# Modulation in steps of two slabs at every second place, and choice tables held in PSUM

## The chip, the cores and the metric

One core of a Trainium2 chip runs the whole program in one launch. The metric is the device time in microseconds (us), median of several executions. Before: 2350.81 us, the median of 3 executions from 2339.59 to 2353.79.

## What is computed

A two-layer backbone over 256 latent tokens (stream x) and 256 context tokens (stream c), width 1024. Each layer mixes tokens with four mixers (windowed attention, gated delta rule, latent attention, retention) and then channels: a dense SwiGLU in layer 0, the best two of eight experts in layer 1. Every sub-layer is modulated by rows that come from a product with `w_mod`:

```python
for layer in range(DEPTH):
    mod_x = (silu_c @ w_mod[layer] + b_mod[layer])[:, None, :]
    mod_c = silu_cc @ w_mod[layer] + b_mod[layer]
    sh1_x, sc1_x, g1_x, sh2_x, sc2_x, g2_x = jnp.split(mod_x, 6, axis=-1)
...
logits = (x @ w_router).astype(jnp.float32)
top_val, top_idx = lax.top_k(logits, TOP_K)
gates = jax.nn.softmax(top_val, axis=-1)
combine = jnp.sum(jax.nn.one_hot(top_idx, N_EXPERTS, dtype=jnp.float32) * gates[..., None], axis=1)
for e in range(N_EXPERTS):
    out = out + combine[:, e:e + 1].astype(x.dtype) * swiglu(x, w_gate[e], w_up[e], w_down[e])
```

## The kernel before, in words

**Long products.** Weights arrive as float32 slabs of 256 rows by 512 columns (512 KB, tile `raw`, five buffers, all loads issued on SP's queue). ScalarE rounds each half to `hi` (lines 200 and 225), VectorE forms the rest `lo` (lines 201 and 226), and TensorE makes three products of the parts (lines 183 to 185). A dense SwiGLU works through seven hidden groups of 512: four slabs of the gate weights (`fg_dram`), two times two of the up weights (`fu_dram`), two times two of the down weights (`fd_dram`). Results are summed in PSUM tiles `acc`, which come from two rings of two banks.

**Modulation between them.** The product with `w_mod` has 24 chunks of 512 columns over both layers. Four chunks are made at the start by `mod`; the other 20 (8 in layer 0, 12 in layer 1) are made in small steps between the slabs of the long products. A step is one `w_mod` slab of 256 rows: `mod_part` (line 285 on) loads it into a buffer of `raw` (line 287) and multiplies it into a PSUM tile `modp` (line 292; 8 calls, which the trace shows as 16 matmul records). VectorE then copies (line 325) or adds (line 327) `modp` to the row tile `mrow` in SBUF. After four steps `mod_out` turns the row (line 297) and adds the bias (line 298). `tick`, which the loops over slabs call at fixed places, takes one step from the list `Fill.steps`; `need_mod` takes steps at once until a chunk is done. `modp` takes its bank from the ring of `acc` that the running product does not use. A dense hidden group has four places, so one chunk is made in each.

**Route.** After the last output projection, `route` (line 1549 on) makes the router's logits `lg`, finds the best two of eight experts per token, and ranks the tokens of each expert. The tables are 128 x 2 x 8 or smaller, in SBUF: `lg` (lines 1563 and 1586), `top` (1574), `eq` (1577), `first` (1579), `hot` (1581), their sum `sel` (1587), the counts `prk` by two matmuls (1589, 1591), and `rank` (1592). `pick` compares `rank` with a row of numbers and gives the selection matrix `oh` (1649); `gather` (1661) multiplies with it the normed tokens, split into `hnh` and `hnl`. The parts `hnl` are made by GpSimd (line 1569) while VectorE makes the choice. `weights` (lines 1597 to 1606: `dl`, `w`, `cw`, `cwt`) makes the experts' weights beside it. Then come the experts: 1 MB slabs `eraw` in nine buffers, split on lines 1624 and 1625, products `gu` and `pd`.

**What sets the order.** A list scheduler places each engine's instructions in advance; work inside `soon()` has priority, `mod_step` and `weights` have none. Each engine works strictly in the placed order, and so does SP with its loads.

Of the kernel before, what the change touches and what calls it, by code (L numbers as in the profile page):

```python
# [11 lines left out]
F32 = mybir.dt.float32  # L12
# [3 lines left out]
OP = mybir.AluOpType  # L16
# [9 lines left out]
OFF = 1024.0  # L26
# [44 lines left out]
def bc(ap, pos, n):  # L71

    a = list(ap.ap)
    a.insert(pos, [0, n])
    return bass.AP(tensor=ap.tensor, offset=ap.offset, ap=a)
# [3 lines left out]
def tile_backbone(ctx: ExitStack, tc: tile.TileContext, x, ctxs, cT, w_mod, w_in, w_out, w_q_up, w_kv_up,  # L79
                  fg, fu, fd, router, mg, mu, md, rows, cols, cst, fnorm, out):  # L80
    nc = tc.nc
    V, S, T, G = nc.vector, nc.scalar, nc.tensor, nc.gpsimd
# [39 lines left out]
    class Thread:  # L122
# [5 lines left out]
        def ps(self, name="acc"):  # L128
            return pp.tile([128, 512], F32, name=name, tag=self.psum[0], bufs=self.psum[1])
# [32 lines left out]
    def soon():  # L162

        return tc.high_priority(offset=6000)

    def hv(ap, h=4):
        return ap.rearrange("p (h d) -> p h d", h=h)
# [117 lines left out]
    def mod_part(l, n, a, p, k0, k1):  # L285
        r = raw.tile([128, 2, 512], F32, name="raw", tag="raw")
        nc.sync.dma_start(r, w_mod[l, a * 256:(a + 1) * 256, n * 512:(n + 1) * 512].rearrange(
            "(k p) c -> p k c", p=128))
        for j in range(2):
            k = a * 2 + j  # L290
            for g in range(4):
                T.matmul(p[32 * g:32 * g + 32, 0:128], sct[:, k, :], r[:, j, g * 128:(g + 1) * 128],
                         start=k == k0, stop=k == k1, skip_group_check=True)

    def mod_out(l, n, row, bank=ps):
        q = bank("modc")
        T.transpose(q[:, 0:128], row, ident)
        V.tensor_tensor(MOD[l][:, 4 * n:4 * n + 4, :], hv(q[:, 0:128])[:, :, 0:2],
                        bc(CL[l]["b_mod"][:, 4 * n:4 * n + 4], 2, 2), op=OP.add)
# [20 lines left out]

    def mod_step(l, n, a):
        p = ps("modp")
        mod_part(l, n, a, p, 2 * a, 2 * a + 1)
        if a == 0:
            V.tensor_copy(mrow, p[:, 0:128])
        else:
            V.tensor_tensor(mrow, mrow, p[:, 0:128], op=OP.add)

    class Fill:

        steps, out = [], None

    def put_fill(l, chunks):
        Fill.steps += [(l, n, a) for n in chunks for a in range(4)]

    def tick():
        if Fill.out:
            mod_out(*Fill.out, mrow)
            Fill.out = None
        if Fill.steps:  # L340
            l, n, a = Fill.steps.pop(0)
            mod_step(l, n, a)
            if a == 3:
                Fill.out = l, n

    def need_mod(l, n):
        while Fill.out or any(st[0] == l and st[1] <= n for st in Fill.steps):
            tick()

    SI = {"x": 0, "c": 1}  # L350

    def modcol(l, kind, s):
        return MOD[l][:, kind * 8:kind * 8 + 8, SI[s]]
# [1011 lines left out]
    first = []  # L1365
# [67 lines left out]
    def squares(n, junk):  # L1433
        for t in range(2):
            S.activation(junk("junk"), H["x", t][:, n * 512:(n + 1) * 512], AF.Square,
                         accum_out=ss[:, n * 2 + t:n * 2 + t + 1])

    def turned(n, psum, sbuf):
        us = []
        for k2 in (2 * n, 2 * n + 1):  # L1440
            p = psum("utp")
            for j in range(2):
                for t in range(2):
                    T.transpose(p[:, j * 256 + t * 128:j * 256 + t * 128 + 128],
                                H["x", t][:, (2 * k2 + j) * 128:(2 * k2 + j + 1) * 128], ident)
            us.append(sbuf("u"))
            if k2 % 2:
                V.tensor_copy(us[-1], p)
            else:
                S.copy(us[-1], p)  # L1450
        return us

    def logits(n, us, acc):
        for i in range(4):
            k = 4 * n + i
            for t in range(2):
                o_ = i % 2 * 256 + t * 128
                T.matmul(acc[:, t * 8:t * 8 + 8], us[i // 2][:, o_:o_ + 128], rt[:, 1, k, :],
                         start=i == 0 and t == 0, stop=i == 3, skip_group_check=True)
# [55 lines left out]
    def pt_(name):  # L1515
        return ptr.tile([128, 512], F32, name=name, tag="tr")
# [4 lines left out]
    def sh_(name, dtype=F32):  # L1521
        return ew.tile([128, 512], dtype, name=name, tag="w")

    def e3(name, dtype=F32):
        return e0.tile([128, 2, NE], dtype, name=name, tag=name)

    def col2(name):
        return e0.tile([128, 2], F32, name=name, tag=name)

    def norms(ss):  # L1530
        ms = small(ST, 2, "ms")
        V.tensor_tensor(ms, ss[:, 0:2], ss[:, 2:4], op=OP.add)  # L1532
        V.tensor_scalar(ms, ms, 1.0 / D, EPS, op0=OP.mult, op1=OP.add)  # L1533
        return rsq(ST, ms, 2)
# [5 lines left out]
    rank, sel, cw = e3("rank"), e3("sel", F32R), e3("cw")  # L1540
# [8 lines left out]
    def route():  # L1549

        cnt = sh_("cnt", F32R)
        S.copy(cnt[:, 0:128], C["strict"])
        S.copy(cnt[:, 128:256], ones)
        squares(1, sh_)
        plg = pt_("plg")
        logits(1, turned(1, pg_, sh_), plg)
        r = norms(ss)
        V.tensor_scalar(fa[1], H["x", 1], r[:, 1:2], None, op0=OP.mult)
        lg0, lgr = e3("lg0"), e3("lgr")
        for t in range(2):  # L1560
            V.scalar_tensor_tensor(lgr[:, t], lga[:, t], r[:, t:t + 1], lsh, op0=OP.mult, op1=OP.add)
        for t in range(2):
            V.scalar_tensor_tensor(lg0[:, t], plg[:, t * 8:t * 8 + 8], r[:, t:t + 1], lgr[:, t], op0=OP.mult, op1=OP.add)
        S.mul(fa[0], H["x", 0], r[:, 0:1])
        for a in range(2):
            cc = slice(a * 512, a * 512 + 512)
            for t in (1, 0):
                S.copy(hn[0][a][t], fa[t][:, cc])
                G.tensor_tensor(hn[1][a][t], fa[t][:, cc], hn[0][a][t].bitcast(F32), op=OP.subtract)
        hot, top = [], []  # L1570
        cur = lg0
        for i in range(2):
            m = col2(f"top{i}")
            V.tensor_reduce(m, cur, axis=AX.X, op=OP.max)
            q = e3(f"eq{i}")
            for t in range(2):
                V.scalar_tensor_tensor(q[:, t], cur[:, t], m[:, t:t + 1], C["rev8"], op0=OP.is_equal, op1=OP.mult)
            f = col2(f"first{i}")
            V.tensor_reduce(f, q, axis=AX.X, op=OP.max)
            oh = e3(f"hot{i}")  # L1580
            V.tensor_tensor(oh, bc(C["rev8"], 1, 2), bc(f, 2, NE), op=OP.is_equal)
            hot.append(oh)
            top.append(m)
            if i == 0:
                cur = e3("lg1")
                V.scalar_tensor_tensor(cur, oh, -3e38, lg0, op0=OP.mult, op1=OP.add)
        V.tensor_tensor(sel, hot[0], hot[1], op=OP.add)
        prk = pt_("prk")
        T.matmul(prk[:, 0:16], cnt[:, 0:128], sel.rearrange("p t e -> p (t e)"), start=True, stop=False,
                 skip_group_check=True)  # L1590
        T.matmul(prk[:, 8:16], cnt[:, 128:256], sel[:, 0], start=False, stop=True, skip_group_check=True)
        V.scalar_tensor_tensor(rank, sel.bitcast(F32), -OFF, hv(prk[:, 0:16], 2), op0=OP.mult, op1=OP.add)
        return hot, top, cnt

    def weights(hot, top, cnt):
        dl = col2("dl")
# [42 lines left out]
                beats.remove(b)  # L1639
                b[1]()  # L1640

    def pick(e, rnd):

        oh = sh_("oh", F32R)
        rk = rank
        if rnd:
            rk = e3("rank1")
            V.tensor_scalar(rk, rank, -128.0, None, op0=OP.add)
        V.tensor_tensor(oh.rearrange("p (t i c) -> p t i c", t=2, i=2), bc(bc(C["iota"], 1, 2), 1, 2),
                        bc(rk[:, :, e:e + 2], 3, 128), op=OP.is_equal)  # L1650
        return oh
# [23 lines left out]
    def back(oh):  # L1675

        pt = pt_("oht")
        ohf = oh.bitcast(F32)
        for i in range(2):
            for t in range(2):  # L1680
                T.transpose(pt[:, i * 256 + t * 128:i * 256 + t * 128 + 128],
                            ohf[:, t * 256 + i * 128:t * 256 + i * 128 + 128], ident)
        ohT = eg.tile([128, 512], F32R, name="ohT", tag="ohT")
        S.copy(ohT, pt)
        return ohT
# [127 lines left out]
        finish(prev, acc)  # L1813

    with soon():
        routed = route()
        oh = pick(0, 0)
        X = [gather(oh, k2, k2 % 2 == 0) for k2 in range(4)]
        ohT = [back(oh)]
        gate_rows(gated, modcol(1, 5, "x"), 1.0, pt_("gatep"), sh_("gate8")[0:8, 0:128], g2)  # L1820
# [66 lines left out]
```

## Time and profile before

| | us |
|---|---|
| median of 3 executions | 2350.81 |
| lowest, highest | 2339.59, 2353.79 |
| profiled execution: time | 2351.19 |
| profiled execution: span from first to last instruction | 2349.4 |
| TensorE busy, VectorE busy, ScalarE busy in the span | 2253.5, 1889.0, 1451.3 |
| mean granted TensorE clock | 0.978 of full speed |

The profile is one execution. Times of rows are in us from the start of its span. PE is TensorE's matmuls, PEld its weight loads, DVE VectorE, ACT ScalarE, POOL GpSimd, SPq SyncE's DMA queue. Matmuls overlap their neighbours, so what one costs is read from start to start, not from its duration.

### The profile page before, as it was taken

Reading aid. Unit: us, or ns where it says so; the run is one execution under the profiler, and the core shown is the slowest. Engines: PE = TensorE matmul, PEld = TensorE weight load, DVE = VectorE, ACT = ScalarE, POOL = GpSimd, SP = SyncE. Lnnn points to the kernel's source line nnn. Section 1 sums busy time; section 2 is a strip of 40 time slices with the busy share of each in tenths; the row PEclk is TensorE's granted clock in tenths of the full one; section 3 lists DMA queues with packets and bytes.
Section 4 is the critical chain, followed back from the end, with each engine's and each line's share of the span. In section 5 each row is a group of like instructions: output and inputs, shape, how many; then the busy total and the mean of one; then the engine's idle time right before and its main releaser. Section 6 shows DMA issues by size and latency. Waiting matters only on the chain. (4 is left out here: it accounts for less than half of the span.)

```text
span 2349.4 us, 40053 instructions
## 1 busy us (share of the span) xinstructions
PE 2253.5 (96%) x14158; PEld 1857.6 (79%) x14158; DVE 1889.0 (80%) x4160; ACT 1451.3 (62%) x2899; POOL 18.5 (1%) x38
## 2 busy tenths in 40 slices
PE   6899999999999999999999899999999999999997
PEld 5667878888888888897777688888878887878785
DVE  5766878676777785578866799989998999999997
ACT  4434463344454463345445699888778877778875
POOL 0000000000000000000000000000000000000000
PEclk9899999999999997999999899999999999999999
DMA  8674454436676666465534499999999999979993
GB/s 299 220 218 127 150 184 147 139 110 213 222 218 208 202 212 184 140 185 162 147 108 153 166 373 358 368 330 342 366 354 342 337 365 362 364 278 357 356 371 130
DMA packets 363490, 579.53 MB, mean 247 GB/s; under 512 B 40864, under 2 KB 120976, under 8 KB 363280
## 3 DMA queue, kind: packets, MB, share of 16 engines
q1 hardware_dynamic: 361104, 568.50, 72.1%
q0 software_dynamic: 2176, 8.39, 1.0%
q8 instruction: 113, 1.85, 0.3%
q14 instruction: 97, 0.79, 0.1%
HBM read 568.37 MB, written 8.46 MB: 246 GB/s over the span
## 5 line engine op out<-in xcount | busy, mean ns | idle before, releaser
L1625 DVE TENSOR_TENSOR elo<-eraw,ehi 128x512 fp32r<-128x512 f32 x1344 | 834.7, 685 | 43.3 <-ACT ehi L1624 42.3
L1624 ACT CAST ehi<-eraw 128x512 fp32r<-128x512 f32 x1344 | 743.4, 621 | 27.2 <-PE gu L185 8.0
L200 ACT CAST hi<-raw 128x512 fp32r<-128x512 f32 (+3 forms) x408 | 245.0, 602 | 349.1 <-PE acc L185 180.0
L184 PE MATMUL gu<-elo,xhi 128*128 128x512 f32 x896 | 356.5, 398 | 3.8 <-DVE elo L1625 3.6
L201 DVE TENSOR_TENSOR lo<-raw,hi 128x512 fp32r<-128x512 f32 (+3 forms) x408 | 267.1, 666 | 114.8 <-ACT hi L200 110.4
L183 PE MATMUL gu<-ehi,xhi 128*128 128x512 f32 x896 | 357.5, 399 | 0.2 <-ACT xhi L225 0.2
L185 PE MATMUL gu<-ehi,xlo 128*128 128x512 f32 x896 | 353.3, 394 | 0.0
L183 PE MATMUL acc<-uh,hi 128*128 128x256 f32 x1072 | 312.0, 291 | 2.8 <-DVE pl L882 2.4
L184 PE MATMUL acc<-ul,hi 128*128 128x256 f32 x1072 | 308.4, 288 | 2.6 <-DVE ul L226 2.6
L185 PE MATMUL acc<-uh,lo 128*128 128x256 f32 x1072 | 307.5, 287 | 0.7 <-DVE lo L201 0.7
L183 PEld LDWEIGHTS acc<-uh,hi 128*128 128x128 f32 x1072 | 206.3, 192 | 14.8 <-issue 11.7
L184 PEld LDWEIGHTS acc<-ul,hi 128*128 128x128 f32 x1072 | 206.7, 193 | 6.4 <-DVE ul L226 2.8
L185 PEld LDWEIGHTS acc<-uh,lo 128*128 128x128 f32 x1072 | 206.6, 193 | 4.0 <-issue 1.5
L184 PEld LDWEIGHTS gu<-elo,xhi 128*128 128x128 f32 x896 | 168.6, 188 | 46.0 <-DVE elo L1625 7.8
L183 PEld LDWEIGHTS gu<-ehi,xhi 128*128 128x128 f32 x896 | 168.5, 188 | 41.2 <-ACT ehi L1624 0.6
L185 PEld LDWEIGHTS gu<-ehi,xlo 128*128 128x128 f32 x896 | 168.6, 188 | 39.7
L184 PE MATMUL pd<-elo,ehh 128*128 128x512 f32 x448 | 181.2, 404 | 0.1
L183 PE MATMUL pd<-ehi,ehh 128*128 128x512 f32 x448 | 177.1, 395 | 0.0
L185 PE MATMUL pd<-ehi,ehl 128*128 128x512 f32 x448 | 176.8, 395 | 0.0
L225 ACT CAST hi<-raw 128x512 fp32r<-128x512 f32 x156 | 96.6, 619 | 107.3 <-PE acc L184 87.4
L183 PE MATMUL acc<-hi,uh 128*128 128x512 f32 (+3 forms) x368 | 143.9, 398 | 14.3 <-ACT uh L225 7.4
L184 PE MATMUL acc<-lo,uh 128*128 128x512 f32 (+3 forms) x368 | 144.4, 393 | 2.4 <-DVE lo L201 2.3
(417 smaller groups left out, 3412.5 us busy)
## 6 DMA issues: line engine op xcount, KB each, us to landing
eraw<-md_dram SPq DMA_DIRECT2D x112, 1024.0 KB, 6.9
eraw<-mg_dram SPq DMA_DIRECT2D x108, 1024.0 KB, 6.9
eraw<-mu_dram SPq DMA_DIRECT2D x108, 1024.0 KB, 6.3
raw<-w_mod_dram SPq DMA_DIRECT2D x96, 512.0 KB, 4.3
raw<-fg_dram SPq DMA_DIRECT2D x56, 512.0 KB, 3.9
raw<-fu_dram SPq DMA_DIRECT2D x56, 512.0 KB, 4.1
raw<-fd_dram SPq DMA_DIRECT2D x56, 512.0 KB, 4.1
raw<-w_in_dram SPq DMA_DIRECT2D x50, 512.0 KB, 3.6
```

The source lines that it names most:

```text
L183: T.matmul(o_ap, lh, rh, start=start, stop=False, skip_group_check=skip)
L184: T.matmul(o_ap, lh, rl, start=False, stop=False, skip_group_check=skip)
L185: T.matmul(o_ap, ll, rh, start=False, stop=stop, skip_group_check=skip)
L200: S.copy(hi[:, :w], r[:, j, :w])
L201: V.tensor_tensor(lo[:, :w], r[:, j, :w], hi[:, :w].bitcast(F32), op=OP.subtract)
L225: S.copy(dst_hi, src)
L1624: S.copy(hi, rr_[:, j])
L1625: V.tensor_tensor(lo, rr_[:, j], hi.bitcast(F32), op=OP.subtract)
```

## The change

A step of the modulation takes two slabs: two loads, 16 matmul calls into one `modp` tile, one copy or add into `mrow`. A chunk has two steps in place of four. `tick` does nothing at every second call; `need_mod` passes `now=True` and skips no call. In `route`, `lg` of both rounds, `first`, the second `hot` and the first `rank` become columns of the PSUM tiles `plg` and `prk`; `rank` and the second `hot` are copied to SBUF after the first `pick`.

```diff
     def mod_step(l, n, a):
         p = ps("modp")
-        mod_part(l, n, a, p, 2 * a, 2 * a + 1)
+        for b in (a, a + 1):
+            mod_part(l, n, b, p, 2 * a, 2 * a + 3)
         if a == 0:
             V.tensor_copy(mrow, p[:, 0:128])
...
-        Fill.steps += [(l, n, a) for n in chunks for a in range(4)]
+        Fill.steps += [(l, n, a) for n in chunks for a in (0, 2)]
-    def tick():
+    def tick(now=False):
+        Fill.wait = not (Fill.wait or now)
+        if Fill.wait:
+            return
...
-            if a == 3:
+            if a == 2:
                 Fill.out = l, n
...
-            tick()
+            tick(True)
...
-        lg0, lgr = e3("lg0"), e3("lgr")
+        lg0, lgr, lg1, fm, hot1 = hv(plg[:, 32:48], 2), e3("lgr"), hv(plg[:, 64:80], 2), plg[:, 96:100], hv(plg[:, 128:144], 2)
...
-            f = col2(f"first{i}")
+            f = fm[:, 2 * i:2 * i + 2]
...
-            oh = e3(f"hot{i}")
+            oh = hot1 if i else e3("hot0")
...
-                cur = e3("lg1")
+                cur = lg1
...
-        V.scalar_tensor_tensor(rank, sel.bitcast(F32), -OFF, hv(prk[:, 0:16], 2), op0=OP.mult, op1=OP.add)
-        return hot, top, cnt
+        rk = hv(prk[:, 32:48], 2)
+        V.scalar_tensor_tensor(rk, sel.bitcast(F32), -OFF, hv(prk[:, 0:16], 2), op0=OP.mult, op1=OP.add)
+        return hot, top, cnt, rk
...
-        routed = route()
-        oh = pick(0, 0)
+        *routed, rk0 = route()
+        oh = pick(0, 0, rk0)
+        V.tensor_copy(rank, rk0)
+        hot1 = e3("hot1")
+        V.tensor_copy(hot1, routed[0][1])
+        routed[0][1] = hot1
```

TensorE, in a dense hidden group (`acc` is a sum of the long products, `modp` the modulation). Before, among the products with gate or up weights:

```order
L183 MATMUL acc<-uh,hi 128x256
L184 MATMUL acc<-ul,hi 128x256
L185 MATMUL acc<-uh,lo 128x256
L292 MATMUL modp<-raw,sct 32x128 x8
L183 MATMUL acc<-uh,hi 128x256
L184 MATMUL acc<-ul,hi 128x256
```

and after, among those with down weights:

```order
L183 MATMUL acc<-hi,hh 128x512
L184 MATMUL acc<-lo,hh 128x512
L185 MATMUL acc<-hi,hl 128x512
L292 MATMUL modp<-raw,sct 32x128 x16
L183 MATMUL acc<-hi,hh 128x512
L184 MATMUL acc<-lo,hh 128x512
```

The first is one of four stretches of 8 in a group, the second one of two stretches of 16. Over the whole program there are 93 stretches of modulation in TensorE's order before and 58 after: 51 and 27 in layer 1, 37 and 26 in layer 0, and 5 in the start, which is not changed.

SP's queue over one dense hidden group. Before:

```order
L193 DMA raw<-fg_dram 128x2x512 x2
L287 DMA raw<-w_mod_dram 128x2x512
L193 DMA raw<-fg_dram 128x2x512 x2
L212 DMA raw<-fu_dram 128x4x256
L287 DMA raw<-w_mod_dram 128x2x512
L212 DMA raw<-fu_dram 128x4x256 x2
L287 DMA raw<-w_mod_dram 128x2x512
L212 DMA raw<-fu_dram 128x4x256
L193 DMA raw<-fd_dram 128x2x512 x3
L287 DMA raw<-w_mod_dram 128x2x512
L193 DMA raw<-fd_dram 128x2x512
```

and after:

```order
L193 DMA raw<-fg_dram 128x2x512 x4
L212 DMA raw<-fu_dram 128x4x256
L287 DMA raw<-w_mod_dram 128x2x512 x2
L212 DMA raw<-fu_dram 128x4x256 x3
L193 DMA raw<-fd_dram 128x2x512 x3
L287 DMA raw<-w_mod_dram 128x2x512 x2
L193 DMA raw<-fd_dram 128x2x512
```

The four `w_mod` loads of a group stand in two pairs, each in two of the five `raw` buffers at once.

VectorE in the route, from the second `eq` to the selection matrix `oh` (`cs` holds the constants). Before:

```order
L1597 TENSOR_TENSOR dl<-top_15643,top_15632 128x2
L1579 TENSOR_REDUCE first_15648<-eq_15645 128x2
L1581 TENSOR_TENSOR hot_15650<-cs_15568,first_15648 128x16
L1600 TENSOR_SCALAR w_15741<-dl 128x2
L1587 TENSOR_TENSOR sel<-hot_15639,hot_15650 128x16
L1601 RECIPROCAL w_15741<-w_15741 128x2
L1602 TENSOR_TENSOR w_15742<-w_15741,dl 128x2
L1604 TENSOR_TENSOR cw<-hot_15639,w_15741 128x16
L1592 SCALAR_TENSOR_TENSOR rank<-sel,prk 128x16
L1605 TENSOR_TENSOR cwt<-hot_15650,w_15742 128x16
L1649 TENSOR_TENSOR oh<-cs_15568,rank 128x512
```

and after:

```order
L1604 TENSOR_TENSOR dl<-top_15560,top_15551 128x2
L1585 TENSOR_REDUCE plg<-eq_15562 128x2
L1587 TENSOR_TENSOR plg<-cs_15488,plg 128x16
L1607 TENSOR_SCALAR w_15659<-dl 128x2
L1593 TENSOR_TENSOR sel<-hot_15557,plg 128x16
L1827 COPY hot_15575<-plg 128x16
L1608 RECIPROCAL w_15659<-w_15659 128x2
L1599 SCALAR_TENSOR_TENSOR prk<-sel,prk 128x16
L1609 TENSOR_TENSOR w_15660<-w_15659,dl 128x2
L1611 TENSOR_TENSOR cw<-hot_15557,w_15659 128x16
L1656 TENSOR_TENSOR oh<-cs_15488,prk 128x512
L1825 COPY rank<-prk 128x16
```

The second `w` and `cw`, which stood ahead of the rank, now stand between it and `oh`, in place of `cwt`; `dl` keeps its place ahead of the second `first`.

## Rows read from the trace of the kernel before

**Rows 1.** The page: TensorE's granted clock in 40 slices, in tenths of full speed
```profile
PEclk9899999999999997999999899999999999999999
```

**Rows 2.** Windows by stage: us, PE, PEld, DVE, ACT, POOL busy (instructions), clock, DMA share, GB/s
```profile
60.00:370.00 310.00, 291.46 (x2217) 226.95 (x2216) 224.70 (x750) 144.56 (x379) 0.00 (x0) 0.96 0.56 171
370.00:910.00 540.00, 528.41 (x4251) 463.32 (x4251) 409.53 (x987) 260.23 (x505) 0.46 (x1) 1.00 0.63 192
...
1290.00:1330.00 40.00, 28.96 (x159) 24.57 (x158) 26.85 (x68) 16.75 (x35) 5.68 (x5) 0.83 0.26 90
1330.00:2349.40 1019.40, 999.80 (x4447) 802.98 (x4445) 930.81 (x1528) 827.77 (x1526) 5.04 (x4) 0.99 0.95 338
```

**Rows 3.** Timeline of PE around one modulation step: start, us, engine, line, what, count
```profile
709.52 0.28 PE L184 MATMUL acc<-ul,hi 128*128 128x256 f32 x1
709.64 0.28 PE L185 MATMUL acc<-uh,lo 128*128 128x256 f32 x1
709.85 0.65 PE L292 MATMUL modp<-raw,sct 128*32 128x128 f32 x16
710.42 0.39 PE L183 MATMUL acc<-uh,hi 128*128 128x256 f32 x1
```

**Rows 4.** Timeline of PE: a long unbroken run of modulation at the start
```profile
39.99 1.95 PE L292 MATMUL modp<-raw,sct 128*32 128x128 f32 x64
```

**Rows 5.** Instructions on mrow: count, ns min/median/max, first and last start
```profile
L327 DVE TENSOR_TENSOR mrow<-mrow,modp x60: 266/280/291, 69.3 to 993.9; 128x128 f32<-128x128 f32 x60
```

**Rows 6.** Waits of PE, 60 to 370 us: us in total, times, longest
```profile
PE modp L292 <- DVE mrow L325: 1.4, 1, 1.4
PE modp L292 <- DMA raw<-w_mod_dram: 1.3, 2, 0.8
```

**Rows 7.** Waits of PE, 370 to 910 us
```profile
PE acc L183 <- DVE mrow L327: 3.0, 1, 3.0
```

**Rows 8.** Loads: the page's DMA issues (KB each, us to landing), and SP's timeline
```profile
raw<-w_mod_dram SPq DMA_DIRECT2D x96, 512.0 KB, 4.3
...
698.33 0.37 SPq L287 DMA_DIRECT2D raw<-w_mod_dram  x1
```

**Rows 9.** Timeline of DVE in the route
```profile
1311.50 0.36 DVE L1561 SCALAR_TENSOR_TENSOR lgr<-lga,rsq_y,lsh 128x8 f32<-128x8 f32 x2
1311.83 0.36 DVE L1563 SCALAR_TENSOR_TENSOR lg<-plg,rsq_y,lgr 128x8 f32<-128x8 f32 x2
...
1312.42 1.44 DVE L1577 SCALAR_TENSOR_TENSOR eq<-lg,top,cs 128x8 f32<-128x8 f32 x2
...
1314.10 0.99 DVE L1581 TENSOR_TENSOR hot<-cs,first 128x16 f32<-128x16 f32 x1
1315.12 1.18 DVE L1586 SCALAR_TENSOR_TENSOR lg<-hot,lg 128x16 f32<-128x16 f32 x1
1316.34 0.17 DVE L1574 TENSOR_REDUCE top<-lg 128x2 f32<-128x16 f32 x1
1316.55 1.11 DVE L1577 SCALAR_TENSOR_TENSOR eq<-lg,top,cs 128x8 f32<-128x8 f32 x2
1317.58 0.15 DVE L1597 TENSOR_TENSOR dl<-top,top 128x2 f32<-128x2 f32 x1
...
1318.96 0.17 DVE L1592 SCALAR_TENSOR_TENSOR rank<-sel,prk 128x16 f32<-128x16 f32 x1 [0.31 <-PE prk L1591]
...
1319.16 0.69 DVE L1649 TENSOR_TENSOR oh<-cs,rank 128x512 fp32r<-128x512 f32 x1
```

**Rows 10.** Timeline of POOL in the route
```profile
1312.57 4.93 POOL L1569 TENSOR_TENSOR hnl<-fa,hnh 128x512 fp32r<-128x512 f32 x4 [9.19 <-ACT hnh L1568]
```

**Rows 11.** Timeline of PE in the route
```profile
1318.33 0.38 PE L1589 MATMUL prk<-sel,cnt 128*128 128x16 f32 x1 [7.81 <-DVE sel L1587]
...
1320.00 0.77 PE L1661 MATMUL gat<-oh,hnh 128*128 128x256 f32 x2 [1.08 <-DVE oh L1649]
```

**Rows 12.** A window inside the last dense groups of layer 0, columns as in rows 2
```profile
915.00:951.00 36.00, 36.00 (x242) 29.99 (x242) 9.46 (x21) 8.39 (x21) 0.00 (x0) 0.50 0.33 109
```

More of the change, by code (lines that the diff above doesn't have):

```diff
@@ L329, in tile_backbone @@
     class Fill:
-        steps, out = [], None
+        steps, out, wait = [], None, False
     def put_fill(l, chunks):
-        Fill.steps += [(l, n, a) for n in chunks for a in range(4)]
-    def tick():
+        Fill.steps += [(l, n, a) for n in chunks for a in (0, 2)]
[3 more added lines that the diff above has]
+            return
         if Fill.out:
@@ L1640, in beat, with pick @@
                 b[1]()
-    def pick(e, rnd):
+    def pick(e, rnd, rk=None):
         oh = sh_("oh", F32R)
-        rk = rank
+        rk = rk or rank
         if rnd:
```

## The prediction

> **What bounds the kernel now.** I read the windows by stage first, then the waits of PE in each stage, then the timeline of one modulation step and of the route, and last the granted clock.
>
> The windows [rows 2] show three regimes. From 60 to 370 us, layer 0's mixers, PE is busy 291.5 of 310 us: it is the bound most of the time, with small holes. From 370 to 910 us, the dense SwiGLU, PE is busy 528.4 of 540 us at full clock, DVE 409.5, and DMA engines 63%: what PE no longer has to do there comes off the time nearly one for one. From 1330 us on the experts run with every engine full (PE 999.8 and DVE 930.8 of 1019.4, DMA 95%); the change touches nothing there, so this stage only starts earlier or later. Between them, from 1290 to 1330 us, is the route: PE is busy 29.0 of 40 us, and its one long wait is 7.81 us for `sel` [rows 11]. That is a chain of short DVE instructions, and its length counts fully.
>
> **The change part by part: fewer bursts on PE.** One step interrupts the long product as follows [rows 3]: the matmul before it starts at 709.64, the one after it at 710.42, 0.78 us apart, where neighbours stand 0.12 us apart (709.52 to 709.64). A step costs 0.66 us. Its 16 records do not explain this by themselves: without the 0.27 us that the last one takes to run out, they start within 0.38 us, 0.025 each, and in the unbroken run of 64 it is (1.95 - 0.27) / 63 = 0.027 each [rows 4]. So 16 more records in the same burst cost 0.40 to 0.43 us, and the entry and exit, 0.25 us or so, are paid once. A pair costs 1.06 to 1.09 us in place of 1.32: it saves 0.23 to 0.26, and I take 0.25.
>
> How many pairs really merge, the order tells: 51 stretches become 27 in layer 1, 37 become 26 in layer 0. Layer 1's are spread over the dense groups, where PE is the bound: 24 x 0.25 = 6.0 us. Layer 0's stand in the mixers, where PE has holes, so I count half: 11 x 0.25 / 2 = 1.4 us. Bounds: nothing, if every entry and exit already lies in a wait, and 35 x 0.26 = 9.1 us if all count.
>
> **Fewer additions on DVE.** Of 60 additions into `mrow`, 0.28 us each [rows 5], 40 go: 11.2 us of DVE time. DVE is idle a quarter of the dense stage [rows 2], so by itself this is worth nothing; PE's long products hide it, and without that cover it would be worth up to 11.2. But an addition also holds the bank that it reads, and has no priority in DVE's order: PE waited 3.0 us for one [rows 7] and 1.4 us for a copy [rows 6]. With half as many evacuations I take half of these 4.4 us: 2.2. Bounds: 4.4 if both go, and minus 4.4 if two more such waits come in the new order. The wait is PE's, and the products behind it on PE wait too.
>
> **Two loads at once.** The pair occupies two of the five `raw` buffers. The load issued at 698.33 [rows 8] is used at 709.85 [rows 3], 11.5 us later, and lands after 4.3 us: some 7 us of slack. A pair gives its two buffers back together, so the slab that follows three slabs later is asked for later than now; three slabs of PE work remain to cover it (24 matmuls each at 0.12 us, 2.9 us a slab), 8.7 us against one landing of 4.3 and part of a second. I cost it at nothing. SP's queue holds the same loads, only moved past two or three slabs. In the mixers the cover is thinner: PE waited twice there for a `w_mod` load, 1.3 us in all [rows 6]. What it costs if the cover is gone is the slower rival below. The skipped places move no deadline: a chunk still takes four places, and its row is turned one active place later, at most two places.
>
> **The route.** Four DVE steps last far longer than their size: the first `eq` pair 1.44 us, `hot` 0.99, the next `lg` 1.18, the second `eq` pair 1.11, while a pair of the same form just before took 0.36 and single ones take 0.17 [rows 9]. All four lie in the 4.93 us in which POOL makes `hnl`, in four instructions of 1.23 us [rows 10], and all read two SBUF tensors; the reduction `top`, with one input, takes 0.17 in the midst of it. Each slow one ends near an end of a POOL instruction (1313.8, 1315.0, 1316.3, 1317.5). So a DVE instruction with two SBUF inputs waits for POOL's running instruction here. The change moves one input of each of the four into PSUM: 1.44 - 0.36 + 0.99 - 0.17 + 1.18 - 0.17 + 1.11 - 0.36 = 3.66 us less. [...]
>
> But the time saved moves other instructions into POOL's stretch. `dl`, two SBUF inputs and still ahead of the second `first`, now started at 1317.58, just clear of POOL. It would be due at 1317.58 - 3.66 = 1313.92, and POOL's next end is 1315.03: it waits 1.11 us, and `first`, `hot` and `sel` wait behind it. Then the rank comes at about 1318.96 - 2.55 = 1316.4, and behind it stand the second `w` and `cw`, two SBUF inputs each, ahead of `oh`. The last POOL instruction ends at 1317.50; with 0.06 and 0.2 us for the two, `oh` starts at about 1317.76 in place of 1319.16. The route gains 1.4 us, not 3.66. Bounds: 3.66 less two instructions of 0.17 is 3.3 if these do not wait; nothing if POOL is slowed in turn. The copies of the rank and of `hot` to SBUF, 0.17 each, lie behind `oh` or in the wait for `prk`. `plg` and `prk` hold their two banks longer, but `plg` is free before `oh`, and `prk` 0.2 us after it, while the eight products of the first gather tile, 0.77 us for two of them [rows 11], take longer than that.
>
> [...] On this trace a pair with a PSUM input lasts 0.36 us like the pair with SBUF inputs before it [rows 9], so the sum has no term for it. [...]
>
> **The sum**, against the profiled execution's own 2351.19 us (span 2349.4 and 1.8 around it): 6.0 + 1.4 + 2.2 + 1.4 = 11.0 us less, 2340.2. That execution lies 0.4 us above the median of the runs shown, so the forecast is **2340 us**, faster by 0.47%. A measurement of this kernel tells about 1%, 23.5 us, from no change: this is within it.
>
> **The rivals.** [...]
>
> *PE waits for the second load* (the slower end). A pair runs in one burst, and its second half cannot start before its second slab has landed; the long products behind it stand still. If each of the 40 pairs waits as the two waits in the mixers did, 0.65 us [rows 6], that is 26 us: 2366, slower than before. It decides from 11 / 40 = 0.28 us a pair. For it: twice the data is due at one place. Against it: the 7 us of slack.
>
> *The change doesn't do what it says.* If PE's entry and exit are covered by other waits, and POOL's stretch catches `dl`, `w` and `cw` for all that was freed, only some of the waits for `mrow` go: 2349.
>
> **How the numbers follow.** The forecast 0.57 (its own range 2332 to 2346), the slow clock gone 0.14, the change without effect 0.18, waits for loads or longer slow stretches 0.11. The unknown bounds add up to 9.1 + 4.4 + 3.3 = 16.8 us less, 2334, and to 4.4 us more without any gain, 2356. The range 2321 to 2357 takes in these, the clock's rival and the near part of the slower one. Faster by over 1%, below 2327.3: most of the clock's rival, 0.13. Slower by over 1%, above 2374.3, needs 0.86 us at every pair: 0.03. Within 1%: 0.84.
>
> **What would show it.** Right: 20 additions into `mrow`; bursts of 32 records spanning about 1.2 us from start to start of their neighbours; PE busy less by 5 to 9 us in layer 1's dense groups; the route's slow four at 0.17 to 0.4 us, `dl` or the second `w` at about 1 us, `oh` 1.4 us earlier from the end of the output projection. Wrong: PE waits for `w_mod` loads of more than 10 us after the first 60, ScalarE's `hi` waiting for `raw`, or half-clock stretches whose sum differs by more than 20 us from before.

## The result, and the profile after

| | before | after |
|---|---|---|
| median, us | 2352.31 (18 executions, 2330.19 to 2369.12) | 2328.95 (18 executions, 2310.5 to 2354.25) |
| ratio | | 0.9892, 95% interval 0.986 to 0.9924 |
| profiled execution: time, span, clock | 2351.19, 2349.4, 0.978 | 2316.41, 2314.6, 0.986 |

Faster by about 1.1%, 23.4 us. The forecast was 2340 us with a range of 2321 to 2357: the range held it, the direction was right, and the median lies 11 us below the forecast.

First what the change did to the row tile. The instructions of `mrow` after, by line (ns: shortest, median, longest):

```profile
L326 DVE COPY mrow<-modp x20: 279/284/292, 66.9 to 905.4; 128x128 f32<-128x128 f32 x20
L328 DVE TENSOR_TENSOR mrow<-mrow,modp x20: 227/281/290, 82.6 to 953.9; 128x128 f32<-128x128 f32 x20
```

Twenty additions are left of the 60 in [rows 5], at the same 0.28 us; with the 20 copies that makes 40 evacuations of `modp` in place of 80. One step in TensorE's timeline (columns as in [rows 3]):

```profile
657.35 0.28 PE L184 MATMUL acc<-ul,hi 128*128 128x256 f32 x1
657.47 0.28 PE L185 MATMUL acc<-uh,lo 128*128 128x256 f32 x1
657.68 1.08 PE L292 MATMUL modp<-raw,sct 128*32 128x128 f32 x32
658.69 0.39 PE L183 MATMUL acc<-uh,hi 128*128 128x256 f32 x1
```

Its neighbours start 657.47 and 658.69, 1.22 us apart; less the 0.12 of undisturbed neighbours a pair costs 1.10, where two steps of [rows 3] cost 1.32. Two waits of TensorE from 60 to 1300 us (us in total, times, longest):

```profile
PE prk L1595 <- DVE sel L1593: 5.7, 1, 5.7
PE modp L292 <- DMA raw<-w_mod_dram: 4.2, 3, 2.4
```

The wait for `sel` was 7.81 [rows 11]. No wait for `mrow` is left of the 3.0 and 1.4 us in [rows 6, 7]. For `w_mod` loads TensorE waits somewhat longer than before, 4.2 us in three waits against 1.3 in two. The route on VectorE, and GpSimd's four instructions beside it, against [rows 9, 10]:

```profile
1278.98 0.50 DVE L1569 SCALAR_TENSOR_TENSOR plg<-plg,rsq_y,lgr 128x8 f32<-128x8 f32 x2
...
1279.73 4.93 POOL L1575 TENSOR_TENSOR hnl<-fa,hnh 128x512 fp32r<-128x512 f32 x4 [9.19 <-ACT hnh L1574]
...
1279.73 0.36 DVE L1583 SCALAR_TENSOR_TENSOR eq<-plg,top,cs 128x8 f32<-128x8 f32 x2
...
1280.34 0.17 DVE L1587 TENSOR_TENSOR hot<-cs,plg 128x16 f32<-128x16 f32 x1
1280.54 0.18 DVE L1592 SCALAR_TENSOR_TENSOR plg<-hot,plg 128x16 f32<-128x16 f32 x1
...
1280.96 0.36 DVE L1583 SCALAR_TENSOR_TENSOR eq<-plg,top,cs 128x8 f32<-128x8 f32 x2
1281.24 1.00 DVE L1604 TENSOR_TENSOR dl<-top,top 128x2 f32<-128x2 f32 x1
1282.16 0.17 DVE L1585 TENSOR_REDUCE plg<-eq 128x2 f32<-128x16 f32 x1
1282.36 0.18 DVE L1587 TENSOR_TENSOR plg<-cs,plg 128x16 f32<-128x16 f32 x1
1282.51 0.96 DVE L1607 TENSOR_SCALAR w<-dl 128x2 f32<-128x2 f32 x1
1283.38 0.16 DVE L1593 TENSOR_TENSOR sel<-hot,plg 128x16 fp32r<-128x16 f32 x1
...
1284.30 0.37 DVE L1609 TENSOR_TENSOR w<-w,dl 128x2 f32<-128x2 f32 x1
...
1284.69 0.68 DVE L1656 TENSOR_TENSOR oh<-cs,prk 128x512 fp32r<-128x512 f32 x1
```

The four slow steps last 0.36, 0.17, 0.18 and 0.36; `dl` lasts 1.0, as forecast; and the first `w`, which the forecast had at its own length, lasts 0.96. The second `w` (line 1609) lasts 0.37 and ends at 1284.67, with the last of GpSimd's four (1284.66), and `oh` follows at once, as forecast. `oh` starts 12.96 us behind the start of the last output product (1271.73), before 14.59 (1304.57 to 1319.16).

**How the runs are compared.** The 18 executions of the changed kernel spread over 44 us. The spread is one of clock: with h, the time that TensorE spent at half clock (the clock records of the two traces hold 1.0 and 0.5 and no other level; taken so for all executions, h = 2 x (1 - clock) x span), the spans lie on a line, 0.417 us of span for each us of h, with 1.9 us of scatter. Below, "at no half clock" is the mean of span - 0.417 h over all executions of a kernel:

| kernel | executions | h, mean | at no half clock | its own "before" |
|---|---|---|---|---|
| before | 29, 29, 23, 11 | 114, 108, 113, 122 | 2304.4, 2302.6, 2302.5, 2302.2 | |
| after | 18 | 103 | 2287.9 | 2304.4 (other runs) |

So some 16.5 us of the 23.4 are there at equal time at half clock; against the other three sets of before it is 14.3 to 14.7. The rest goes with the clock: by the line, the median span of before (2350.5) stood at 111 us of half clock, that of after (2327.1) at 94, and 17 x 0.417 = 7. With single executions from 60 to 200 us, the means of 103 and of 108 to 122 do not tell whether the change itself lowers h.

### The profile page after: what moved, and what is told of

Its sections match the earlier page's. It is cut to its first block, busy times and chain, and to the rows that moved or that the text cites. A ratio compares the mean times of both kernels' runs of the same rounds, so it can differ in the third digit from the quotient of the medians.

```text
span 2314.6 us, 39987 instructions
## 1 busy us (share of the span) xinstructions
PE 2224.3 (96%) x14158; PEld 1845.8 (80%) x14158; DVE 1878.9 (81%) x4122; ACT 1451.1 (63%) x2899; POOL 18.5 (1%) x38
## 3 DMA queue, kind: packets, MB, share of 16 engines
q8 instruction: 113, 1.85, 0.3%
## 5 line engine op out<-in xcount | busy, mean ns | idle before, releaser
L226 DVE TENSOR_TENSOR lo<-raw,hi 128x512 fp32r<-128x512 f32 x156 | 107.5, 690 | 57.1 <-ACT hi L225 55.2
```

What stands on the lines that cost most here:

```text
L226: V.tensor_tensor(dst_lo, src, dst_hi.bitcast(F32), op=OP.subtract)
```

## The experiments

The theory, *bursts*: the gain is the entries and exits of `modp` bursts that merged, and a little from the route. A burst is an unbroken stretch of `modp` products. Rivals: *evacuations* (VectorE's 11 us and the banks that it holds), *the order's luck* (each change makes the list scheduler write another order, and the waits in it happen to be fewer), *loads*.

**The parts by themselves.** `route_only` is the changed kernel with the old modulation (one slab a step, no place skipped), `mod_only` the changed kernel with the old route.

```diff
# route_only, against the changed kernel
-        for b in (a, a + 1):
-            mod_part(l, n, b, p, 2 * a, 2 * a + 3)
+        mod_part(l, n, a, p, 2 * a, 2 * a + 1)
...
-        Fill.steps += [(l, n, a) for n in chunks for a in (0, 2)]
+        Fill.steps += [(l, n, a) for n in chunks for a in range(4)]
```

> The change without its modulation part: TensorE's order up to the route is that of the kernel before. Theory: 1.6 us faster than the kernel before at the same sum of half-clock time, all of it between the end of the last product and the selection matrix (13.0 us in place of 14.6); the sum of half-clock time is spread as in the kernel before, about 107 us in the profile. Rival (route): over 5 us faster.

> The change without its route part: modulation in pairs, tables of the route in SBUF as before. TensorE's order up to the route is that of the changed kernel. Theory (bursts and clock): up to the end of the last output projection it behaves as the changed kernel (1272 us at 65 us of half clock, 0.4 to 0.5 us later for each further us at half clock), and the route takes as long as before: from the end of the last product to the selection matrix 14.6 us, not 13.0. In all 1.6 us slower than the changed kernel at the same sum of half-clock time. Rival (route): the route's part is worth more than its own stretch shows, and this kernel stays within 5 us of the kernel before.

Measured: `route_only` 2347.22, ratio 0.9991 (0.9953 to 1.0029), at no half clock 2302.2, 2.2 us below before. `mod_only` 2331.89, ratio 0.9943 (0.9899 to 0.9986), 2289.3, 15.1 below. They add up to 17.3, the whole is 16.5. In TensorE's timeline from the first to the last down product, 48 bursts that cost 34.5 us in before (each from start to start of its neighbours, less 0.12) are 26 that cost 27.0 in `mod_only`; between 60 us and the first down product 40 bursts and 36.6 us are 27 and 32.9. But these 7.5 + 3.7 = 11.2 us less are not all entries and exits. The two dearest bursts of the dense groups in before (2.19 us at 631.8, 1.85 at 857.5) stand ahead of a wait for `mod` and one for `cn`, and `mod_only` has both waits too, away from its bursts. Before, 370 to 910 us, and `mod_only`, 380 to 1050 us:

```profile
PE cnt L604 <- DVE cn L594: 1.6, 2, 1.4
PE gatep L358 <- DVE mod L298: 1.2, 1, 1.2
```

```profile
PE gatep L363 <- DVE mod L298: 1.6, 1, 1.6
PE cnt L609 <- DVE cn L599: 1.3, 2, 1.0
```

What merging alone takes away is, by an estimate, 35 entries and exits at the 0.22 that a pair saves (1.32 less 1.10): 7.7 of the 15.1.

**The slow clock's stretch is not the order's.** `route_only` has TensorE's order of before up to the route, and no 37 us stretch at half clock at 913 as in [rows 12]; it has one of 27 us at 476 (one execution each). The same kernel's h ran from 70 to 186 us over 29 executions of before.

**Fewer evacuations, the same bursts.** `half_evac` is before, with every second copy or addition left out, 40 of the 80, so that half of each modulation sum is missing from the result.

```diff
-        if a == 0:
+        if a == 1:
             V.tensor_copy(mrow, p[:, 0:128])
-        else:
+        elif a == 3:
```

> The kernel before, with 40 of its 60 evacuations of modp left out: VectorE copies the second slab's bank of each chunk and adds the fourth's, so the other half of each modulation sum is left out of the result; every product of TensorE is still made, in 98 bursts (before: 93). All times here are spans with 0.417 us taken off for each us at half clock, by which before stands at 2304.4 and the kernel with the modulation part alone at 2289.3. Theory 'bursts' (about 11 of these 15 us are entries and exits of bursts that merged): 2300 to 2306, since no burst goes and only waits for mrow can, 3 us at most. Rival 'evacuations' (banks held and VectorE's 11 us): 2297 or less. Rival 'the order's luck': outside both, or over 2307.

Measured: 2341.87, ratio 0.9983 (0.9959 to 1.0007); at no half clock 2300.0, 2.5 below its own before. That is the lower edge of what *bursts* has; *evacuations* wanted 2297 or less. Its order differs from that of before in 2283 of TensorE's 16578 places.

**Pairs that do not share a sum.** `pair_two_sums` keeps the pairs of loads at every second place, and gives each slab its own `modp` and its own copy or addition.

```diff
-    def mod_step(l, n, a):
-        p = ps("modp")
-        for b in (a, a + 1):
-            mod_part(l, n, b, p, 2 * a, 2 * a + 3)
+    def mod_step(l, n, a2):
+        for a in (a2, a2 + 1):
+            p = ps("modp")
+            mod_part(l, n, a, p, 2 * a, 2 * a + 1)
```

> The modulation part alone (route of before), steps of two slabs at every second place, but each slab in its own modp with its own copy or addition: 60 evacuations, pairs of loads, 85 bursts where the pair in one sum has 58. Theories 'bursts' and 'evacuations': no better than 2299 at no half clock, 2299 to 2306. Rival 'loads and places' (the gain is from loading in pairs at every second place): 2288 to 2293.

Measured: 2385.3, ratio 1.016 (1.0107 to 1.0213); at no half clock 2305.8, 16.5 above `mod_only`. The pairing of loads and the skipped places are worth nothing by themselves. This run does not tell bursts from evacuations, since it gives back both.

**Luck of the order.** `before_phase` is before with all modulation steps one place later, `phase` is `mod_only` with all of them one place earlier.

```diff
# before_phase
+    def tick(now=False):
+        if Fill.skip and Fill.steps and not now:
+            Fill.skip = False
+            return
# phase
-        steps, out, wait = [], None, False
+        steps, out, wait = [], None, True
```

> The kernel before, with the first modulation step that has work skipped once, so that all later steps fall one place later; the same bursts, additions and loads, 1142 of PE's places read otherwise. Theories 'bursts' and 'evacuations': 2301 to 2308 at no half clock (before 2304.4). Rival 'the order's luck' (the 15 us between before and the modulation part alone lie in which waits an order happens to have): over 6 us away from 2304.4, as the like shift of the new kernel was 5.5 us away from its own.

> The change without its route part, with the pairs at the first and third place of each four instead of the second and fourth: the same bursts, loads and evacuations, set one place earlier, and another order on all engines. Theory (bursts and evacuations): within 3 us of mod_only at the same half-clock sum. Rival (luck of the order): more than 5 us away, and then as much of the change's gain may be the order's.

Measured: `before_phase` 2376.88, ratio 1.0073 (1.0028 to 1.0118), 2307.8 at no half clock, 5.3 above its own before; `phase` 2344.28, ratio 0.9984 (0.9949 to 1.002), 2294.8, 5.5 above `mod_only`. So an order is worth some 5 us, more than the 3 us that the theory allowed `phase`; both shifts were to the slower side. In `phase` a wait shows that before has too [rows 7] and `mod_only` has not; TensorE's waits from 380 to 1075 us:

```profile
PE acc L183 <- DVE mrow L326: 3.9, 1, 3.9
PE acc L184 <- DVE ul L226: 2.6, 1, 2.6
PE gatep L363 <- DVE mod L298: 2.3, 1, 2.3
```

With either phase the pairs are ahead: 2289.3 and 2294.8 against 2304.4 and 2307.8. Against before in the same series of runs the modulation part is worth 15.1 us with one phase and 7.8 with the other.

**VectorE's work given back.** Both add 40 additions of 0.28 us to `mod_only`, the 11.2 us that the change took away: `reads_back` ahead of each evacuation, reading the `modp` bank once more, `dve_back` behind it and in SBUF alone.

```diff
# reads_back
+        V.tensor_tensor(mrow2, mrow2, p[:, 0:128], op=OP.add)
# dve_back
+        V.tensor_tensor(mrow2, mrow2, mrow, op=OP.add)
```

> The change without its route part, and each pair's PSUM tile is read twice on VectorE (a second addition into a spare row), so that the 40 additions which the change took away are back, while TensorE's bursts stay merged. Theory (bursts): at the same sum of half-clock time as mod_only within 3 us. Rival (VectorE): the 11.2 us of additions were on the path: 8 to 11 us slower than mod_only at the same sum.

> The change without its route part, with 40 additions of the old size put back on VectorE, but from one SBUF row to another, after each evacuation: the PSUM bank is freed as early as in mod_only. Reads_back, where the added instruction reads the bank, stood 12.7 us above mod_only at the same half-clock sum. Theory (the bank): what reads_back lost is the time that the product's bank ring is held; this kernel stays within 3 us of mod_only at the same sum. Rival (VectorE's time): the 11.2 us themselves are on the path: 9 to 13 us above mod_only.

Measured: `reads_back` 2355.86, ratio 1.003 (0.9992 to 1.0068), at no half clock 2302.0, 12.7 above `mod_only`; `dve_back` 2375.7, ratio 1.005 (0.9999 to 1.0102), 2303.7, 14.4 above. The added ones in `reads_back` (the view leaves out the 2 of `mrow2`):

```profile
L327 DVE TENSOR_TENSOR mrow<-mrow,modp x40: 268/281/291, 66.9 to 982.4; 128x128 f32<-128x128 f32 x40
```

Here *bursts* failed its own test, which wanted `reads_back` within 3 us of `mod_only`, and the bank is not the reason, since the kernel without it loses as much. By the words of both expectations the rival, VectorE's time, came out, with ranges of 8 to 11 and 9 to 13 us that the losses even pass. With the bursts merged and VectorE's work as before, 2.4 us are left of the gain in `reads_back` and none in `dve_back`. But their orders differ from that of `mod_only` in 1580 to 1843 of TensorE's places, and single waits stand in them, as in `dve_back` from 60 to 390 us:

```profile
PE acc L183 <- ACT uh L225: 6.8, 2, 5.1
PE pt L484 <- ACT p L475: 6.4, 2, 6.2
PE retsc L766 <- DVE mod L298: 3.6, 1, 3.6
```

and in `reads_back`, from 380 to 1075 us:

```profile
PE acc L183 <- DVE X L1029: 4.2, 1, 4.2
...
PE acc L183 <- DVE mrow L331: 1.8, 1, 1.8
```

The profiles tell lost entries from lost waits. The table has, from 60 us to the first expert product `gu`, the bursts and TensorE's idle time; then the difference to before that they give (that of idle time, and 0.22 us for each burst more or less); then the difference that was measured at no half clock, to each kernel's own before:

| kernel | bursts | idle, us | the two against before | measured |
|---|---|---|---|---|
| before | 88 | 56.8 | | |
| after | 53 | 52.5 | -12.0 | -16.5 |
| `mod_only` | 53 | 54.5 | -10.0 | -15.1 |
| `phase` | 57 | 59.6 | -4.0 | -7.8 |
| `reads_back` | 62 | 61.3 | -1.1 | -2.4 |
| `dve_back` | 56 | 68.1 | +4.3 | +1.1 |
| `pair_two_sums` | 80 | 64.1 | +5.6 | +3.3 |
| `half_evac` | 93 | 52.9 | -2.8 | -2.5 |
| `before_phase` | 94 | 60.8 | +5.4 | +5.3 |
| `route_only` | 88 | 54.8 | -1.9 | -2.2 |

With one profile of each kernel the two come within 5.1 us of the measured differences, and within 0.3 where no bursts merge and no loads pair. The saving by merged bursts is thus there in `reads_back` and `dve_back` too; against `mod_only` these lose 6.8 and 13.6 us to idle time. Whether the 11.2 us of additions made these waits or the new order did is open: no run adds one and keeps the order. Open, too, are the 1 to 5 us by which every kernel with paired loads is better than the sum of the two.

**Larger steps.** `four` takes all four slabs of a chunk in one step at every fourth place, with no addition left.

```diff
-        for b in (a, a + 1):
-            mod_part(l, n, b, p, 2 * a, 2 * a + 3)
+        for b in range(4):
+            mod_part(l, n, b, p, 0, KD - 1)
```

> The change without its route part, taken one step further: all four slabs of a chunk at every fourth place, one burst, one copy, no addition. Theory (bursts): in the dense groups 12 bursts of 64 records at 1.95 us instead of 24 of 32 at 1.10: 3 us less there, 1 us less in layer 0, and 20 evacuations fewer: 4 to 6 us below mod_only at the same half-clock sum. Rival (loads): four of the five buffers are held by one chunk, TensorE waits for the slab behind it: 5 us or more above mod_only, with waits for w_mod loads or for ScalarE's hi over 10 us in the dense stage.

Measured: 2366.48, ratio 1.0089 (1.006 to 1.0117), 2308.1 at no half clock, 18.8 above `mod_only`. Here the slower rival of the prediction has come true: four of the five `raw` buffers are due at one place. Two bursts of 16 records in its timeline,

```profile
641.20 0.91 PE L292 MATMUL modp<-raw,sct 128*32 128x128 f32 x16 [1.06 <-DMA raw<-w_mod_dram]
642.47 1.08 PE L292 MATMUL modp<-raw,sct 128*32 128x128 f32 x16 [0.36 <-DMA raw<-w_mod_dram]
```

and its waits for loads from 380 to 1080 us,

```profile
PE modp L292 <- DMA raw<-w_mod_dram: 7.7, 16, 1.4
```

show it: 16 waits for loads, 7.7 us, where in `mod_only` they come to less than 0.4 us in the like stretch. Its 18 bursts there cost 47.4 us in place of 27.0, some of it at half clock (20 us from 641 on). Of the steps tried, two slabs is where merging stops paying.

**The weights behind `oh`.** `late_weights` is the changed kernel with `dl` and all that follows it made to wait for `oh` by one small instruction that reads `oh`.

```diff
         dl = col2("dl")
+        V.tensor_scalar(dl, oh[:, 0:2].bitcast(F32), 0.0, None, op0=OP.mult)
         V.tensor_tensor(dl, top[1], top[0], op=OP.subtract)
```

> The changed kernel, with the experts' weights (dl, w, cw) made to wait for the selection matrix. Theory (two engines wait for each other at SBUF): dl lasts 1.00 us and w 0.96 us in the changed kernel only because GpSimd works then; moved behind, they leave the chain, first, hot and sel follow each other in 0.2 us, and the selection matrix comes 10.9 us after the end of the last product, not 13.0: 2.0 us less in all. Rival (the tables' latency in PSUM, or the counts' matmuls, set the time): 12.6 us or more, no gain over 0.4 us.

Measured: 2323.45, ratio 0.9869 (0.9825 to 0.9914), 2286.6 at no half clock, 1.3 below the changed kernel. `oh` starts 11.12 us behind the start of the last output product (1290.76 to 1301.88), 1.84 earlier than in the changed kernel; the rival wanted 12.6 or more. From the second `eq` on:

```profile
1300.00 0.36 DVE L1583 SCALAR_TENSOR_TENSOR eq<-plg,top,cs 128x8 f32<-128x8 f32 x2
1300.39 0.18 DVE L1585 TENSOR_REDUCE plg<-eq 128x2 f32<-128x16 f32 x1
1300.61 0.18 DVE L1587 TENSOR_TENSOR plg<-cs,plg 128x16 f32<-128x16 f32 x1
1300.82 0.17 DVE L1593 TENSOR_TENSOR sel<-hot,plg 128x16 fp32r<-128x16 f32 x1
```

Nothing on the way to `sel` waits any longer, so what waited in the changed kernel were `dl` and the two `w` (lines 1607 and 1609) alone.

**`w` in PSUM.** `w_psum` puts the first `w` into the tile `prk`, which its order places behind `oh`; `dl` stays where it was.

```diff
-        return hot, top, cnt, rk
+        return hot, top, cnt, prk[:, 64:66], rk
...
-        w1, w2 = col2("w1"), col2("w2")
+        w2 = col2("w2")
```

> The changed kernel with w written into the PSUM tile prk in place of SBUF, by which the order puts it behind oh; dl stays ahead of first. Theory (each of dl and w waits for the end of a GpSimd instruction by itself): dl still lasts about 1.0 us, sel follows at its own length, and oh starts 0.8 to 1.0 us earlier, 12.0 us behind the end of the last output product where the changed kernel has 12.96. Rival (the wait passes to the next VectorE instruction with SBUF operands, hot or sel): oh within 0.3 us of 12.96.

Measured: one execution, 2328.93 at a clock of 0.970. `oh` starts 11.91 us behind the last output product's start (1302.15), 1.05 earlier than in the changed kernel (both numbers of the expectation, too, count from that product's start, not its end):

```profile
1311.66 0.99 DVE L1604 TENSOR_TENSOR dl<-top,top 128x2 f32<-128x2 f32 x1
1312.58 0.17 DVE L1585 TENSOR_REDUCE plg<-eq 128x2 f32<-128x16 f32 x1
1312.77 0.18 DVE L1587 TENSOR_TENSOR plg<-cs,plg 128x16 f32<-128x16 f32 x1
1312.99 0.17 DVE L1593 TENSOR_TENSOR sel<-hot,plg 128x16 fp32r<-128x16 f32 x1
...
1314.06 0.69 DVE L1656 TENSOR_TENSOR oh<-cs,prk 128x512 fp32r<-128x512 f32 x1
```

The wait of `w` was its own and did not pass on to `hot` or `sel`. Of the 1.05 us some 0.8 are this wait, and 0.2 that of the second `w`, which is behind `oh` now, too. But the kernel stood far lower than that at no half clock, at 2268.9, and so it was run again:

> The same kernel as w_psum, many executions. Its one execution so far stood at 2268.9 at no half clock, 19 below the changed kernel, 17 of it in the experts' stage, where neighbouring products were 229 ns apart in place of 234. Theory 'that execution' (no kernel part explains it): the executions lie at 2285 to 2288, the 0.9 us of the route below the changed kernel, and the profile shows 234 ns. Rival 'the kernel' (its order or its place of w changes the experts' products): all lie at 2267 to 2272, the profile shows 229 ns.

Measured: 2314.92 (six executions, 2298.7 to 2342.18), ratio 0.9836 (0.978 to 0.9893); at no half clock 2270.9, each of the six between 2268.6 and 2273.9: 31.3 below before, 17.0 below the changed kernel. It is the kernel's, and the fastest of all that ran. TensorE's down products of the experts in the changed kernel,

```profile
1419.79 0.40 PE L185 MATMUL pd<-ehi,ehl 128*128 128x512 f32 x1
...
1421.66 0.40 PE L184 MATMUL pd<-elo,ehh 128*128 128x512 f32 x1
```

are the first and the ninth of a run, 1.87 us for eight, 0.234 each; in `w_psum` the same

```profile
1449.16 0.39 PE L183 MATMUL pd<-ehi,ehh 128*128 128x512 f32 x1
...
1450.97 0.39 PE L185 MATMUL pd<-ehi,ehl 128*128 128x512 f32 x1
```

take 1.81, 0.226 each. Over the stage, the first gate product to the last:

```profile
L183 PE MATMUL gu<-ehi,xhi x896: 390/396/628, 1290.5 to 2283.7; 128*128 128x512 f32 x180
```

993.2 us in the changed kernel, and in `w_psum`

```profile
L183 PE MATMUL gu<-ehi,xhi x896: 388/392/628, 1319.8 to 2296.4; 128*128 128x512 f32 x180
```

976.6, 16.6 less (976.2 in the second profile of this kernel). Idle time is the same there, 5.2 us in all three, and 3.4 us less at half clock explain at most 1.7. What differs is hardly the order (25 of TensorE's places, as many as between `mod_only` and the changed kernel, where the pace stays), but the addresses that the program gives its tiles: without the small tile `w` all tiles `eraw`, `ehi` and `elo`, which lie next to it, start 32 bytes further on in each partition (the first `ehi` at byte 188544 in place of 188512). Before, the changed kernel, `mod_only`, `route_only` and `late_weights` all have them at an odd multiple of 32, `w_psum` at a multiple of 64. The dense products with down weights, whose `hi` and `lo` lie at multiples of 64 in every kernel (the first at 68928), run at the faster pace in the changed kernel too, the first and the ninth of one run:

```profile
478.91 0.40 PE L183 MATMUL acc<-hi,hh 128*128 128x512 f32 x1
...
480.73 0.39 PE L185 MATMUL acc<-hi,hl 128*128 128x512 f32 x1
```

1.82 us for eight, 0.2275 each. The addresses fit both contrasts; no kernel shifted them alone, so that they are the cause is argued, not shown, and which of the three tiles counts is open.

## Why the prediction was right, and where it was off

- **Merged bursts**, forecast 6.0 in the dense groups and 1.4 in layer 0's mixers: 35 entries and exits fewer at the 0.22 of a pair are 7.7. This step was right, in mechanism and size. Whether layer 0's count at half, as the forecast has it, or in full is not shown: bursts there hold waits of up to 5.8 us in `mod_only`.
- **Waits for `mrow`**, forecast 2.2: both waits of [rows 6, 7], 4.4 us, are gone in the profiles of the changed kernel and of `mod_only`; in `phase` one is there again at 3.9. As a mean over orders, with bounds of 4.4 both ways, the size fits.
- **VectorE's 11.2 us at nothing**: this step stays open. Taking 40 evacuations out of before gained 2.5 us (`half_evac`), but giving the 11.2 us back to the merged kernel cost 12.7 and 14.4, of which 6.8 and 13.6 are idle time of TensorE. That the cover by long products hides VectorE's work in any order, the runs do not show.
- **Two loads at once at nothing**: nearly right. From 60 us on TensorE waits 4.2 us for `w_mod` loads, before 1.3; the prediction named more than 10 as a sign of error. `four` shows where the slack ends.
- **The route**, forecast 1.4: 1.6 by the profile, 2.2 (with an error of 1.2) by `route_only`. The step on what waits next was right for `dl` (1.0) and for the second `w`, which ended with GpSimd's last instruction ahead of `oh`; what it missed is the first `w`, which lasted 0.96. The rule that the prediction drew from [rows 9], two SBUF inputs, left it out: `w` has one. It waits in the traces all the same: `w` ends at 1283.47, with GpSimd's third `hnl` (1279.73 + 3 x 1.23 = 1283.42), as `dl` does with the second (1282.24 and 1282.19); and the `tensor_scalar` that `late_weights` adds, also with one SBUF input, lasts 1.13 us and ends at 1303.73, when GpSimd's last should end: 1303.69, by an estimate from the changed kernel, whose four last 4.93 us from the start of the first `eq` (here 1298.76). The reduction `top` has one SBUF input, too, and takes 0.17 beside GpSimd [rows 9]; what sets it apart from `w` is not shown. Tables in PSUM were not quite free either: the pair for the first `lg`, which has its input `plg` and its output there, took 0.50 us in place of 0.36 [rows 9].
- **The sum**, 11.0: 14.3 to 16.5 at no half clock. The terms of the modulation part, 9.6 together, lie between the 15.1 of one phase and the 7.8 of the other, so the gap is of the size of an order's luck; no single term is shown to be mis-sized by it. That the median fell 11 us below the forecast is this gap and the clock's 7 us. A gain of over 1% had a chance of 0.13 in the prediction.
- **The slow clock**: that the stretch of [rows 12] goes, a chance of 0.14, was priced as the change's, at 18 us. No run shows the 18 us, which the lower end of the range takes in; by the line of the runs, 0.417 for each us, 36 us at half clock are some 15. `route_only`, with the order of before, lacks the stretch as well, so it is one execution's. In the two profiles h differs by 39 us (106.6 and 67.3), which the prediction named as a sign of error; 16 of the 35 us between the two profiled executions are this, and 7 of the 23 between the medians. Here it helped, which is luck as far as the runs tell; had the sum been compared with one other execution, it could have hidden the whole gain.

## What to carry to other kernels

Short bursts between long products pay for each entry and exit: here joining two saved 0.22 us of 1.32, and it paid until the loads for one place took most of the buffers. Such a gain can be lost again in waits: count the bursts and the idle time of the engine apart. Compare executions at equal time at half clock before a gain of 1% is believed or given up, and move a change by one place to see what its order alone is worth. A small tile added to or taken from a pool moves every tile behind it: look at the pace of the long products after it.

## What the runs showed of the hardware

- **32 bytes, 17 us.** The down products, of 512 columns, stood 0.226 us apart (experts, `w_psum`) and 0.2275 (dense groups) where their tiles start at multiples of 64 bytes, 0.234 where at odd multiples of 32; gate products of the experts 0.231 (`w_psum`, seven steps from 1699.73 to 1701.35) and 0.234; see `w_psum`. The addresses as the cause are argued, not shown: products of `hi` and `lo` with `uh` and `ul`, of 512 columns, stand 0.2325 apart in before and in the changed kernel (medians, 420 to 900 us), though `hi` and `lo` start at multiples of 64 there.
- **Time at half clock differs from run to run by 100 us and more** in one kernel (60 to 160 in 18 executions of the changed one, 75 to 200 in 23 of before), each us costing some 0.42 us. Its mean was higher in three kernels whose profiles show TensorE idle for longer in layer 0's mixers (from 60 us to the first down product): 158, 176 and 164 us with 23.2, 23.2 and 28.6 idle (`before_phase`, `pair_two_sums`, `dve_back`), 93 to 142 with 16 to 21 in the others. That idle time is the cause is not shown: the longest stretch in any profile, 78 us from 206 on, is in `w_psum_again`, with 18.8 us idle. What such a stretch costs, `dve_back` shows; the columns are those of [rows 2]:

```profile
218.00:263.00 45.00, 45.00 (x290) 38.14 (x289) 12.94 (x40) 11.05 (x32) 0.00 (x0) 0.51 0.20 59
```

  PE is busy all of the 45 us at 0.51 and gets 290 matmuls done; in `mod_only` the same 45 us are at 1.00:

```profile
218.00:263.00 45.00, 43.87 (x492) 37.06 (x492) 28.45 (x114) 16.63 (x50) 0.00 (x0) 1.00 0.44 132
```
